# Holding each k copy for a store, and GpSimd's drain for all stores, in a windowed attention kernel

## The chip, the cores and the metric

The kernel runs on one core of a Trainium2 chip. The metric is the device time of that core in microseconds (us), the median of several runs; lower is better. Every run told of here is fast. A single core has no second die to compare with, so fast means that the run lies within 1.5% of the fastest of the same kernel. The runs of the kernel before on one chip agree within 0.13%, and the 95% interval of a ratio below is about ±0.0014, or 1.3 us; a smaller difference between two times isn't clear by itself.

## The reference

Attention within windows of 64 rows; scale is 1536 to the power -0.5:

```
B, S, D, W = 4, 4096, 1536, 64          # q, k, v: float32
logits = einsum('bnwd,bnud->bnwu', q_w, k_w) * scale
attn   = softmax(logits over u)
out    = einsum('bnwu,bnud->bnwd', attn, v_w)   # float32
```

Three inputs of 100.66 MB are read and one output of that size is written. The arithmetic is small beside that.

## The kernel before

A block is 512 rows; there are N = 32. GpSimd asks for all loads but the first q, which are cast to fp16 on the way into SBUF, and for all stores but the last block's, on one DMA queue. When a load has landed, GpSimd copies it to the one buffer that PE reads and asks for the load of two blocks later. PE, the matrix engine, transposes q and k, multiplies them, and multiplies the exponentials with v, reading SBUF and writing PSUM, the two memories on the chip. VectorE and ScalarE copy out of PSUM; their scaled output goes to one of NO = 3 buffers, from which it is stored.

```
    def hand_over(x, u, dst, m, g):
        gp.wait_ge(landed[x][u % NL], 16 * ((u + u % NL) // NL))   # the load has landed
        gp.wait_ge(m, u)                                           # PE is done with the old one
        gp.tensor_copy(out=dst..., in_=landing[x][u % NL]...).then_inc(c_l, 1)
        copies[0] += 1
        gp.wait_ge(c_l, copies[0])
        gp.sem_inc(g, 1)                                           # tell PE
        request(x, u + NL)                                         # the load of block u + 2
...
        for u in range(1, N):
            hand_over("q", u, q16, m_q, g_q)
            hand_over("k", u, k16, m_k, g_k)
            if u + NL == N - 1:
                hand_over("v", u, v16, m_v, g_v)
            gp.wait_ge(m_q, u + 1)
            store(u - 1)                    # adds 16 to d_o[(u - 1) % NO] when landed
            if u + NL != N - 1:
                hand_over("v", u, v16, m_v, g_v)
...     # SyncE issues the two stores of the last block
        gp.drain()
        gp.sem_inc(done, 1)
        sy.wait_ge(done, 1)
        for i in range(NO):                 # SyncE waits for GpSimd's stores
            last = max(u for u in range(N - 1) if u % NO == i)
            sy.wait_ge(d_o[i], 16 * (last // NO + 1))
```

(Cuts are marked with "...", and the comments are added.)

The softmax here doesn't subtract the row's maximum and nothing guards it: scores larger than these inputs give would overflow.

Of the kernel before, what the change touches and what calls it, by code (L numbers as in the profile page):

```python
# [17 lines left out]
def kernel(  # L18
# [20 lines left out]
    N = B * S // UR  # L39
# [11 lines left out]
    def sem(name):  # L51
        sems.append(nc.alloc_semaphore(name))
        return sems[-1]
# [4 lines left out]
    NL = 2  # L58
# [3 lines left out]
    NO = 3  # L62
# [13 lines left out]
    d_o = [sem(f"d_o{i}") for i in range(NO)]  # L76
# [19 lines left out]
    def rows(x, row0, n, r):  # L96
        return x[row0 : row0 + P * n].rearrange("(h p r) d -> p h (r d)", p=P, r=r)

    def slots(t, lo, hi, r):
        return t[:, lo:hi, :].rearrange("p (h r) d -> p h (r d)", r=r)  # L100

    def load(name, u, dst, s):
        src = {"q": qf, "k": kf, "v": vf}[name]
        r = R if name == "v" else SLOTS
        nc.gpsimd.dma_start(
            out=slots(dst, 0, SLOTS, r), in_=rows(src, u * UR, SLOTS, r)
        ).then_inc(s, 16)
# [176 lines left out]
    def store(u):  # L284
        nc.gpsimd.dma_start(
            out=rows(of, u * UR, SLOTS, SLOTS), in_=slots(outs[u % NO], 0, SLOTS, SLOTS)
        ).then_inc(d_o[u % NO], 16)

    def request(x, u):
        if u < N:  # L290
            load(x, u, landing[x][u % NL], landed[x][u % NL])
# [3 lines left out]
    def hand_over(x, u, dst, m, g):  # L295

        gp = nc.gpsimd
        gp.wait_ge(landed[x][u % NL], 16 * ((u + u % NL) // NL))
        gp.wait_ge(m, u)
        gp.tensor_copy(  # L300
            out=dst[:, :, :].bitcast(FP32), in_=landing[x][u % NL][:, :, :].bitcast(FP32)
        ).then_inc(c_l, 1)
        copies[0] += 1
        gp.wait_ge(c_l, copies[0])
        gp.sem_inc(g, 1)
        request(x, u + NL)

    with tc.tile_critical(no_gpsimd_drain=True):

        nc.sync.dma_start(  # L310
            out=slots(outs[0], 0, SLOTS, SLOTS), in_=rows(qf, 0, SLOTS, SLOTS)
        ).then_inc(d_q0, 16)
        load("k", 0, k16, d_k0)
        nc.vector.memset(ident[:, :], 0.0).then_inc(i_d, 1)
        nc.gpsimd.wait_ge(i_d, 1)
        nc.gpsimd.affine_select(
            out=ident[:, :], in_=ident[:, :], compare_op=mybir.AluOpType.not_equal,
            fill=1.0, base=0, pattern=[[-1, P]], channel_multiplier=1,
        ).then_inc(i_p, 1)
        load("v", 0, v16, d_v0)  # L320
        for u in (1, 2):
            for x in "qkv":
                request(x, u)
        nc.gpsimd.wait_ge(d_q0, 16)
        nc.gpsimd.tensor_copy(out=q16[:, :, :], in_=outs[0][:, :, :]).then_inc(c_q, 1)

        nc.vector.memset(ones[:, :], 1.0).then_inc(i_d, 1)
        nc.vector.memset(zeros[:, :], 0.0).then_inc(i_d, 1)
        for et in ets:
            nc.vector.memset(et[:, :, :, :], 0.0).then_inc(i_d, 1)  # L330
        nc.scalar.wait_ge(i_d, 5)
        nc.scalar.activation(zeros[:, 3:4], zeros[:, 0:1], EXP, bias=zeros[:, 0:1], scale=1.0)

        with nc.Fori(0, N, engines=OrderedEngineSet([PE]), head_slot={PE: 0}):
            tensor_unit()
        assert N % NO == 2
        for eng, unit in ((DVE, vector_unit), (ACT, scalar_unit)):
            with nc.Fori(0, N // NO, engines=OrderedEngineSet([eng]), head_slot={eng: 0}):
                for u in range(NO):
                    unit(u)  # L340
            for u in range(N - 2, N):
                unit(u)

        sy = nc.sync
        for j in range(NJ):
            for n in (2, 3):
                sy.sem_inc(f_o[j][n], 1)
        for a in range(2):
            sy.sem_inc(fr[a], NO)
        sy.sem_inc(f_s[-1], 1)  # L350
        sy.wait_ge(i_p, 1)
        sy.wait_ge(i_d, 5)
        sy.wait_ge(c_q, 1)
        sy.sem_inc(g_q, 1)
        sy.sem_inc(g_k, 1)._wait_ge(d_k0, 16)
        sy.sem_inc(g_v, 1)._wait_ge(d_v0, 16)
        for u in range(NO, N):
            sy.wait_ge(d_o[u % NO], 16 * (u // NO))
            for a in range(2):
                sy.sem_inc(fr[a], 1)  # L360

        gp = nc.gpsimd
        for u in range(1, N):
            hand_over("q", u, q16, m_q, g_q)
            hand_over("k", u, k16, m_k, g_k)
            if u + NL == N - 1:

                hand_over("v", u, v16, m_v, g_v)
            gp.wait_ge(m_q, u + 1)
            store(u - 1)  # L370
            if u + NL != N - 1:
                hand_over("v", u, v16, m_v, g_v)


        last = rows(of, (N - 1) * UR, SLOTS, SLOTS)[:, 0, :]
        for i, c in enumerate((1, 3)):
            for a in range(2):
                sy.wait_ge(n_e[a], c)
            sy.dma_start(
                out=last[:, 2 * i * D : 2 * (i + 1) * D],  # L380
                in_=outs[(N - 1) % NO][:, 2 * i : 2 * (i + 1), :].rearrange("p r d -> p (r d)"),
            ).then_inc(d_l[i], 16)
        gp.drain()
        gp.sem_inc(done, 1)
        sy.wait_ge(done, 1)
        for i in range(NO):
            last = max(u for u in range(N - 1) if u % NO == i)
            sy.wait_ge(d_o[i], 16 * (last // NO + 1))
        for i in range(2):
            sy.wait_ge(d_l[i], 16)  # L390
        lo, hi = min(s.num for s in sems), max(s.num for s in sems)
        assert hi - lo + 1 == len(sems)
        sy.sem_clear(range(lo, hi + 1))
# [30 lines left out]
```

## Time and profile before

| | before |
|---|---|
| median, range of 6 runs | 943.35 us, 943.21 to 943.64 |
| span of the profiled run | 941.7 us |
| DMA queue q0, share of 16 engines | 99.7% |
| PE busy | 644.9 us (68%) |
| mean granted PE clock (1 is full speed) | 0.884 |

The prediction below shows the lines that say what bounds the kernel: the DMA queue is full. Three more lines of the page are those of GpSimd's copies. Their columns are line, engine, operation, tiles, shapes and count, then busy time and mean length, then the idle time just before them and what ended most of it:

```profile
L300 POOL COPY v<-vl 128x3072 f32<-128x3072 f32 x31 | 85.2, 2749 | 272.4 <-DMA vl<-in_v_dram 272.4
...
L300 POOL COPY k<-kl 128x3072 f32<-128x3072 f32 x31 | 85.2, 2748 | 102.8 <-DMA kl<-in_k_dram 102.8
L300 POOL COPY q<-ql 128x3072 f32<-128x3072 f32 x31 | 85.0, 2743 | 99.8 <-DMA ql<-in_q_dram 99.8
```

GpSimd waits longest for v, because a store lies between k and v in the queue.

### The profile page before, as it was taken

The page shows a single profiled execution, that of the slowest core. Times are in us where ns is not written, and L with a number is a line of the kernel's source. Part 1 is how long each engine was busy: PE and PEld are TensorE (multiplying, and loading weights), DVE is VectorE, ACT ScalarE, POOL GpSimd, SP SyncE. Part 2 cuts the span into 40 slices and gives each one's busy share as a digit, 9 for nine tenths or more (in the row PEclk, how much of TensorE's full clock was granted, in tenths as well). Part 3 has the DMA queues.
Part 4 walks back from the last instruction along what each step waited for, and adds up shares of the span by engine and source line. Part 5 has one row for each costly group of instructions (what it writes and reads, how often), then busy time and mean ns, then how long its engine had stood idle before and what let it go on. Part 6 is the DMA issues. An engine that isn't in the chain of part 4 may idle for free. (4 is left out here: it accounts for less than half of the span.)

```text
span 941.7 us, 13144 instructions
## 1 busy us (share of the span) xinstructions
PE 644.9 (68%) x5120; PEld 373.5 (40%) x3584; DVE 288.3 (31%) x517; ACT 335.5 (36%) x642; POOL 334.2 (35%) x225
## 2 busy tenths in 40 slices
PE   0877777666766867768666586676776767767683
PEld 0544444433444423445233443334533344334450
DVE  0233333333323332233322233322333223333232
ACT  0344444333333333333333333333333334233331
POOL 4244433344333342333433334333343333443230
PEclk9999999988889788798988999889878889798886
DMA  9999999999999999999999999999999999999997
GB/s 256 219 215 278 265 237 282 283 281 277 231 275 284 280 282 236 266 282 281 283 245 255 283 282 280 256 245 283 282 280 269 233 281 283 282 279 231 273 322 323
DMA packets 22684, 253.35 MB, mean 269 GB/s; under 512 B 2064, under 2 KB 2064, under 8 KB 10256
## 3 DMA queue, kind: packets, MB, share of 16 engines
q0 software_dynamic: 22240, 246.95, 99.7%
q1 hardware_dynamic: 432, 6.29, 1.7%
q14 instruction: 10, 0.08, 0.0%
q8 instruction: 2, 0.03, 0.0%
HBM read 301.99 MB, written 100.66 MB: 428 GB/s over the span
## 5 line engine op out<-in xcount | busy, mean ns | idle before, releaser
L164 PE MATMUL lt<-xq,xk 128*128 128x256 f16 x1536 | 202.6, 281 | 0.0
L300 POOL COPY v<-vl 128x3072 f32<-128x3072 f32 x31 | 85.2, 2749 | 272.4 <-DMA vl<-in_v_dram 272.4
L192 PEld LDWEIGHTS <-et 128*64 128x64 f16 x512 | 40.8, 132 | 331.5 <-issue 317.0
L152 PE MATMUL tp<-ident,q 128*128 128x128 f32 x768 | 109.1, 288 | 80.2 <-DVE xq L228 55.9
L164 PEld LDWEIGHTS lt<-xq,xk 128*128 128x128 f16 x1536 | 152.9, 100 | 26.9
L152 PE MATMUL tp<-ident,k 128*128 128x128 f32 x768 | 125.5, 298 | 54.3 <-PEq L218 37.5
L112 PE MATMUL sp<-ones,et 128*64 128x1 f16 x512 | 52.8, 179 | 146.2 <-PEq L218 126.8
L152 PEld LDWEIGHTS tp<-ident,q 128*128 128x128 f32 x768 | 86.9, 146 | 120.8 <-issue 120.8
L228 ACT COPY xk<-tp 128x512 f32<-128x512 f32 x96 | 59.4, 619 | 199.7 <-ACTq L218 199.7
L152 PEld LDWEIGHTS tp<-ident,k 128*128 128x128 f32 x768 | 96.7, 153 | 71.8 <-issue 69.9
L300 POOL COPY k<-kl 128x3072 f32<-128x3072 f32 x31 | 85.2, 2748 | 102.8 <-DMA kl<-in_k_dram 102.8
L300 POOL COPY q<-ql 128x3072 f32<-128x3072 f32 x31 | 85.0, 2743 | 99.8 <-DMA ql<-in_q_dram 99.8
L245 DVE RECIPROCAL rs<-sp 128x1 f32<-128x1 f32 x128 | 21.3, 166 | 323.9 <-DVEq L218 323.4
L112 PE MATMUL o<-v,et 128*64 128x512 f16 x768 | 118.7, 443 | 0.0
L228 DVE COPY xk<-tp 128x512 f32<-128x512 f32 x96 | 66.4, 692 | 165.4 <-DVEq L218 165.4
L279 ACT ACTIVATE out<-tp,rs 128x512 f32<-128x512 f32 x64 | 44.0, 687 | 177.2 <-ACTq L218 177.2
L269 ACT ACTIVATE et<-lt,zeros 32x128 f16<-32x128 f32 x256 | 91.8, 359 | 39.4 <-ACTq L218 36.1
L228 ACT COPY xq<-tp 128x512 f32<-128x512 f32 x96 | 56.2, 585 | 127.8 <-ACTq L218 127.8
L112 PE MATMUL tp<-v,et 128*64 128x512 f16 x512 | 101.0, 472 | 0.0
L256 DVE TENSOR_SCALAR out<-o,rs 128x512 f32<-128x512 f32 x128 | 90.3, 747 | 28.6 <-DVEq L218 28.1
L228 DVE COPY xq<-tp 128x512 f32<-128x512 f32 x96 | 66.0, 687 | 84.4 <-DVEq L218 84.4
L112 PE MATMUL lt<-v,et 128*64 128x512 f16 x256 | 64.7, 481 | 0.0
(21 smaller groups left out, 217.5 us busy)
## 6 DMA issues: line engine op xcount, KB each, us to landing
out_dram<-out POOLq DMA_DIRECT2D x31, 3072.0 KB, 61.6
ql<-in_q_dram POOLq DMA_DIRECT2D x31, 1536.0 KB, 54.9
kl<-in_k_dram POOLq DMA_DIRECT2D x31, 1536.0 KB, 54.9
vl<-in_v_dram POOLq DMA_DIRECT2D x31, 1536.0 KB, 54.9
out<-in_q_dram SPq DMA_DIRECT2D x1, 3072.0 KB, 16.7
out_dram<-out SPq DMA_DIRECT2D x2, 1536.0 KB, 12.6
k<-in_k_dram POOLq DMA_DIRECT2D x1, 1536.0 KB, 18.0
v<-in_v_dram POOLq DMA_DIRECT2D x1, 1536.0 KB, 24.3
```

What stands on the lines that cost most here:

```text
L112: return nc.tensor.add_instruction(mybir.InstMatmult(name=nc.get_next_instruction_name(), engine=PE, ins=[low(rhs), low(w)], outs=[low(o)] ...
L152: ins = nc.tensor.transpose(tps[g % 2][:, r, j, :], pairs[:, c * P : (c + 1) * P], ident[:, :])
L164: ins = nc.tensor.matmul(lts[h][:, r, :, :], lhsT=keys(c, h, r, w), rhs=queries(c, h, w), start=(c == 0 and w == 0 and r == 0), stop=(c == ...
L192: ld = nc.tensor.ldweights(w[h], tile_position=(0, P // H * h))
L228: copy(out=dst, in_=tps[g % 2][:, :, :, :]).then_inc(f_c[g % 4], 1)
L245: ve.reciprocal(out=rs[:, n : n + 1], in_=sp[:, n : n + 1]).then_inc(n_d, 1)
L256: ins = ve.tensor_scalar_mul(scaled(u, n, j), bank(n, j), scalar1=rs[:, n : n + 1])
L269: ins = sc.activation(ets[h][s, :, :, t], lts[h][s, :, :, t], EXP, bias=zeros[s, 0:1], scale=scale)
L279: ins = sc.activation(scaled(u, n, j), bank(n, j), COPY, bias=0.0, scale=rs[:, n : n + 1])
L300: gp.tensor_copy(out=dst[:, :, :].bitcast(FP32), in_=landing[x][u % NL][:, :, :].bitcast(FP32)).then_inc(c_l, 1)
```

## The change

GpSimd gets a wait before each k copy of blocks 3 to 29: the store that was queued right behind that k must have landed. At the end, the waits for the stores move from SyncE to GpSimd, ahead of its drain, so that GpSimd drains with no store of its own in flight.

```
             hand_over("q", u, q16, m_q, g_q)
+            if NO <= u < N - NL:
+                gp.wait_ge(d_o[u % NO], 16 * (u // NO))
             hand_over("k", u, k16, m_k, g_k)
...
+        for i in range(NO):
+            last = max(u for u in range(N - 1) if u % NO == i)
+            gp.wait_ge(d_o[i], 16 * (last // NO + 1))
         gp.drain()
         gp.sem_inc(done, 1)
         sy.wait_ge(done, 1)
-        for i in range(NO):
-            last = max(u for u in range(N - 1) if u % NO == i)
-            sy.wait_ge(d_o[i], 16 * (last // NO + 1))
```

## The prediction

> **What bounds the kernel now.** I read the page's slices and queues first, to see which resource is never idle; then the timeline of one steady block on GpSimd, to see what each copy waits for; then the tail in stretches of 2 us. A block is 512 rows: 32 blocks, each with a q, a k and a v load and one store of the output.
>
> ```profile
> span 941.7 us, 13144 instructions
> ...
> DMA  9999999999999999999999999999999999999997
> ...
> q0 software_dynamic: 22240, 246.95, 99.7%
> ...
> HBM read 301.99 MB, written 100.66 MB: 428 GB/s over the span
> ```
>
> The sixteen DMA engines are at nine tenths or more in 39 of 40 slices, and GpSimd's one queue q0 fills 99.7% of their time. PE, the busiest compute engine, is at 68%. So this is a transfer-bound kernel, and nothing counts unless it changes how fast the queue moves, lets it run dry, or lengthens an end of the run.
>
> The GpSimd timeline of one block shows the beat of that queue:
>
> ```profile
> 399.06 2.74 POOL L300 COPY q<-ql 128x3072 f32<-128x3072 f32 x1 [3.24 <-DMA ql<-in_q_dram]
> 402.38 0.55 POOL L105 DMA_DIRECT2D ql<-in_q_dram  x1 [0.57 <-POOL q L300]
> 406.39 2.75 POOL L300 COPY k<-kl 128x3072 f32<-128x3072 f32 x1 [3.46 <-DMA kl<-in_k_dram]
> 409.71 0.53 POOL L105 DMA_DIRECT2D kl<-in_k_dram  x1 [0.57 <-POOL k L300]
> 410.23 0.54 POOL L285 DMA_DIRECT2D out_dram<-out  x1
> 420.91 2.75 POOL L300 COPY v<-vl 128x3072 f32<-128x3072 f32 x1 [10.14 <-DMA vl<-in_v_dram]
> ...
> 428.19 2.74 POOL L300 COPY q<-ql 128x3072 f32<-128x3072 f32 x1 [3.23 <-DMA ql<-in_q_dram]
> ...
> 435.52 2.75 POOL L300 COPY k<-kl 128x3072 f32<-128x3072 f32 x1 [3.47 <-DMA kl<-in_k_dram]
> ```
>
> Columns: start, length, instruction, and in brackets the idle time before it with what ended it. Every copy waits for its own landing. Copy to copy: q to k 7.33 us, k to v 14.52, v to q 7.28; a block is 435.52 - 406.39 = 29.13 us. Between k and v the queue holds one more transfer, the store issued just behind that k's request two blocks earlier; so 14.52 is a store plus a load, and the store lands about 14.52 - 7.28 = 7.2 us after k. Each transfer moves 128 x 6144 x 4 B = 3.15 MB on the memory side, 432 GB/s at 7.28 us.
>
> **What the Trainium skill says.** "DMA: Bandwidth & Descriptors", section "Where 436 GB/s comes from", gives 435.2 GB/s as the ceiling of the SBUF ports; the trace's 432 agrees and leaves under 1%. The same page, "Issuing engines are not separate DMA queues", says that DMAs of all issuers run on the same 16 engines; the last two stores, issued by SyncE, do overlap with GpSimd's last one here. "Perfetto Trace Analysis", "DMA Instruction — SWDGE (GPSIMD)", says that the profiled span of a GpSimd DMA is descriptor generation, not data movement; the trace agrees: 0.5 to 0.7 us per issue against tens of us to landing.
>
> ```profile
> out_dram<-out POOLq DMA_DIRECT2D x31, 3072.0 KB, 61.6
> ql<-in_q_dram POOLq DMA_DIRECT2D x31, 1536.0 KB, 54.9
> kl<-in_k_dram POOLq DMA_DIRECT2D x31, 1536.0 KB, 54.9
> vl<-in_v_dram POOLq DMA_DIRECT2D x31, 1536.0 KB, 54.9
> ```
>
> The last figure is the median time from issue to landing. A transfer takes 7.3 us, so a request stands behind about 54.9 / 7.3 = 7.5 transfers: the backlog is nearly two blocks.
>
> **The change, part by part.**
>
> Part 1, the new wait before the k copy, in blocks 3 to 29 (27 times). For block u it waits for the store of block u-3, which is exactly the one queued right behind block u's k. It adds no data and changes no order: GpSimd issues the same transfers in the same sequence. It moves the k copy from k's landing to that store's landing, about 7.2 us later (406.4 to 413.6 in the block shown). What follows from it:
> - The next k request goes out at 416.9 instead of 409.7 and the store behind it at about 417.5 instead of 410.2. Their landings don't move, as the queue before them doesn't. So k's issue to landing should fall from 54.9 to about 54.9 - 7.2 = 47.7 us, the store's from 61.6 to about 54.4; q and v stay at 54.9. A backlog of 47 us is still over six transfers. Cost: 0.
> - The v copy isn't late: GpSimd is done with k and two issues at about 418.0, and v lands at 420.9. The wait moves from v to k: the page's 102.8 us before the k copies should become about 102.8 + 27 x 7.2 = 297, and the 272.4 before the v copies about 272.4 - 194 = 78.
> - PE gets k 7.2 us later. Does it fit in the block? From the same block's timeline of all engines: end of k copy (409.14) to the end of the exponentials (420.67) is 11.5 us; the product with v runs from 423.98 to the first q transpose at 432.34, 8.4; the q transposes run 403.04 to 408.07, and with the last copy out of PSUM to 408.85, 5.8. Sum 25.7 against 29.13: about 3.4 us of slack, and the loop keeps up with the queue. PE's work just moves: today it waits 5.5 us for v and 1.4 us for k (its waits in this block); afterwards the product with v should start when the exponentials end, near 428.0 instead of 424.0, and PE should wait 3 to 4 us before the k transposes. Cost: 0.
>
> Beginning: the early blocks are the ones where PE lags. In block 3, k lands at 86.0, so its store lands near 93, but that block's q transposes end only at 100.64, where the store behind them is issued (the wait of 10.80 us before it). Block 4: store near 122.4, q transposes done at 125.46. The wait is covered. In block 5 the k copy comes at about 151.5, q is done at 148.87, and the slack takes it. Cost: 0.
>
> End: blocks 30 and 31 have no new wait. Block 29's k copy starts near 851.4 instead of 844.22, so its exponentials end near 851.4 + 2.75 + 11.5 = 865.7, and its product with v, which today starts at 861.95, slips 3.7 us. Its slack, and 4.5 us that PE waits today for v of block 30, take that up before block 31: by 888.07 + 2.75 = 890.8 (v of block 30 copied) the delay is about 1 us, by block 31's k nothing. Cost: 0 to 0.5.
>
> Part 2, the waits moved from SyncE to GpSimd ahead of its drain. Today GpSimd drains right after its last copy, 909.92 + 2.75 = 912.7, with three stores still in the queue. Then it will wait for its last store, issued at 905.96 and landing 29.4 us later, at about 935.4. The queue is busy to about 936:
>
> ```profile
> 924.00:926.00 2.00, 1.52 (x16) 0.14 (x2) 1.27 (x3) 1.61 (x3) 0.00 (x0) 1.00 1.00 430
> ...
> 934.00:936.00 2.00, 0.00 (x0) 0.00 (x0) 0.00 (x0) 0.00 (x0) 0.00 (x0) 0.50 0.85 363
> 936.00:938.00 2.00, 0.00 (x0) 0.00 (x0) 0.00 (x0) 0.00 (x0) 0.00 (x0) 0.50 0.17 74
> 938.00:940.00 2.00, 0.00 (x0) 0.00 (x0) 0.00 (x0) 0.00 (x0) 0.00 (x0) 0.50 0.06 25
> ```
>
> (stretch, length, busy time of PE, weight loads, VectorE, ScalarE and GpSimd, then clock, DMA share and GB/s.) SyncE's own last stores, issued at 924.9 and 927.1, take 12.6 us and land near 939.7. So the drain has about 4 us in which it is hidden. No row shows its cost, and no page bears on the drain of a GpSimd that has DMAs out. Cost: 0, perhaps 1 us if it is slow. Nothing is won either, as SyncE waits for the same stores today.
>
> Sum: 0 + 0 + 0 to 0.5 + 0 to 1. I take +0.2: 943.6 us.
>
> **The rivals.**
> 1. The k delay becomes the bound. If all of it stood in the path, 27 x 7.2 = 194 us, so about 1138. For it: k feeds PE, and the wait is in every block. Against: PE waits 6.9 us per block now and the chain sums to 25.7 of 29.13. If my chain were short by 4 us the loss would be 0.6 x 27 = 16 us, still under 2%.
> 2. The queue runs dry, because k and stores are asked for later. For it: the issue really is late. Against: 47 us of backlog where one transfer takes 7.3. It would show as DMA slices under 9.
> 3. The transfers go faster, because GpSimd's copy and issue fall elsewhere. The skill's ceiling bounds it: 402.65 MB / 435.2 GB/s = 925 us (an estimate) without start and tail, while 2% off 943.4 is 924.6. Faster by over 2% is ruled out; 1 to 3 us would be possible.
> 4. The drain after the stores becomes the last thing. If it took over 4 us the end would move by the excess: 1 to 3 us.
>
> **Range and chances.** The three runs before span 0.4 us. Rivals 2 to 4 at their likely sizes give -1 to +2: 942.5 to 945.2. Rival 1 at full size gets most of the 2% for slower; 1% for faster is for what I haven't thought of.
>
> **What would show it.** Right: DMA slices all at 9, a block of 29.1 us, the k wait near 297 and the v wait near 78, k's landing near 47.7. Step "the chain fits" is wrong if blocks are longer than 29.2 and DMA slices fall to 8. Step "the tail absorbs it" is wrong if SyncE's last stores go out later than 927. Step "the drain is hidden" is wrong if the span goes on over 2 us past the last landing. What would make the number wrong is a change of the rate at which the same queue moves, which nothing here foretells.

## The result, and the profile after

The changed kernel takes 945.61 us (median of 6 runs, 945.54 to 946.04) against 943.35. The ratio is 1.0024, with a 95% interval of 1.0011 to 1.0037. By the 2% rule the two are the same; but the loss of 2.3 us is outside the range that was forecast, and clear of noise.

From the page of the changed kernel, the lines that answer to those shown of before:

```profile
span 944.3 us, 13143 instructions
...
DMA  9999999999999999999999999999999999999996
...
q0 software_dynamic: 22240, 246.95, 99.5%
...
HBM read 301.99 MB, written 100.66 MB: 426 GB/s over the span
...
L300 POOL COPY k<-kl 128x3072 f32<-128x3072 f32 x31 | 85.2, 2750 | 304.6 <-DMA out_dram<-out 291.2
...
L300 POOL COPY q<-ql 128x3072 f32<-128x3072 f32 x31 | 85.1, 2745 | 99.3 <-DMA ql<-in_q_dram 99.3
L300 POOL COPY v<-vl 128x3072 f32<-128x3072 f32 x31 | 85.3, 2753 | 83.6 <-DMA vl<-in_v_dram 83.6
...
out_dram<-out POOLq DMA_DIRECT2D x31, 3072.0 KB, 54.7
ql<-in_q_dram POOLq DMA_DIRECT2D x31, 1536.0 KB, 55.1
kl<-in_k_dram POOLq DMA_DIRECT2D x31, 1536.0 KB, 47.6
vl<-in_v_dram POOLq DMA_DIRECT2D x31, 1536.0 KB, 55.2
```

The wait went where it was expected: 304.6 us before k, nearly all ended by a store ("out_dram<-out"), and 83.6 before v. No slice of DMA time fell below 9 before the last. The queue is still full, carries the same packets, and took longer over them.

GpSimd's timeline of the same block shows the k copy 8.0 us later (it was at 406.39), q and v 0.75 us later:

```profile
399.81 2.74 POOL L300 COPY q<-ql 128x3072 f32<-128x3072 f32 x1 [3.23 <-DMA ql<-in_q_dram]
403.13 0.55 POOL L105 DMA_DIRECT2D ql<-in_q_dram  x1 [0.58 <-POOL q L300]
414.41 2.75 POOL L300 COPY k<-kl 128x3072 f32<-128x3072 f32 x1 [10.73 <-DMA out_dram<-out]
...
421.66 2.75 POOL L300 COPY v<-vl 128x3072 f32<-128x3072 f32 x1 [2.86 <-DMA vl<-in_v_dram]
...
428.94 2.74 POOL L300 COPY q<-ql 128x3072 f32<-128x3072 f32 x1 [3.23 <-DMA ql<-in_q_dram]
```

I followed the start of the q copy through all blocks of both traces. The changed kernel is 0.75 us late at block 14, 2.15 at block 28 and 2.51 at block 31. So the loss isn't at the end of the run: it builds up. Up to block 14 it comes in two jumps (about 0.5 us in block 4, at whose start it was 0.37 early, and 0.6 in block 7). From about block 15 on, a block takes about 29.3 us in place of 29.13. The kernel before begins to do the same, but only at block 21.

What grows is the lag of one DMA engine. A transfer is split over sixteen engines, and the trace keeps the sixteen completions of each. Here are those of block 31's q load (worked out from the trace, in us from the span's start):

| | first of 16 | median | last but one | last |
|---|---|---|---|---|
| before | 891.99 | 892.46 | 894.16 | 895.29 |
| after | 892.02 | 892.99 | 895.16 | 897.80 |

The last moved by 2.51 us, as much as the q copy that waits for it, the median by 0.53 and the first by 0.03. A wait for a transfer needs all sixteen, so the one that trails sets the time. The tail shows it too. In stretches of 2 us, the last two columns are the mean share of the sixteen DMA engines and their GB/s. The changed kernel:

```profile
934.00:936.00 2.00, 0.00 (x0) 0.00 (x0) 0.00 (x0) 0.00 (x0) 0.00 (x0) 0.50 0.94 399
936.00:938.00 2.00, 0.00 (x0) 0.00 (x0) 0.00 (x0) 0.00 (x0) 0.00 (x0) 0.50 0.32 135
938.00:940.00 2.00, 0.00 (x0) 0.00 (x0) 0.00 (x0) 0.00 (x0) 0.00 (x0) 0.50 0.07 31
940.00:942.00 2.00, 0.00 (x0) 0.00 (x0) 0.00 (x0) 0.00 (x0) 0.00 (x0) 0.50 0.07 31
```

A share of 0.06 is one engine of sixteen. It moves data alone for 4 us. The line of before for 938 to 940, shown in the prediction, says 0.06 as well: I had read it as the end of the queue and not as one engine by itself.

The packets say where it falls behind. Between 250 and 780 us of the trace's clock, load packets take 474 ns (v) and 926 ns (q, k) in both kernels, alike to 0.05 ns in the mean. Store packets usually take 912 ns, and the first of each engine 925. Of 2304 in that stretch, 50 took over 2% more than 912 before, and 82 after. In the stores of late blocks nearly all of these slow packets follow one another end to start, so they are one engine's. I call what a store's 128 packets take over 912 ns, the 925s left out, its **excess**, and give the mean over the stores of blocks 6 to 25: 128 ns before, 193 after. The difference of 65 ns over the 27 blocks with the wait is 1.8 us of the 2.3 lost. (The same sum, the excess less 128 ns times 27, comes within 0.7 us of what each of the fourteen runs below gained or lost.) The jump of 0.6 us in block 7 comes with slow load packets in that one profile. The profile of e1 below has one of 0.4 a block earlier; whether it comes in every run isn't known.

### The profile page after: what moved, and what is told of

It reads as the page before. It is cut to its first block, busy times and chain, and to the rows that moved or that the text cites. A ratio compares the mean times of both kernels' runs of the same rounds, so it can differ in the third digit from the quotient of the medians.

```text
span 944.3 us, 13143 instructions
## 1 busy us (share of the span) xinstructions
PE 639.5 (68%) x5120; PEld 395.4 (42%) x3584; DVE 287.9 (30%) x517; ACT 334.9 (35%) x642; POOL 334.6 (35%) x225
## 5 line engine op out<-in xcount | busy, mean ns | idle before, releaser
L152 PE MATMUL tp<-ident,k 128*128 128x128 f32 x768 | 150.3, 341 | 126.2 <-PEq L218 117.0
L164 PE MATMUL lt<-xq,xk 128*128 128x256 f16 x1536 | 213.8, 291 | 0.0
L300 POOL COPY k<-kl 128x3072 f32<-128x3072 f32 x31 | 85.2, 2750 | 304.6 <-DMA out_dram<-out 291.2
L152 PEld LDWEIGHTS tp<-ident,k 128*128 128x128 f32 x768 | 116.3, 177 | 146.9 <-issue 144.3
L164 PEld LDWEIGHTS lt<-xq,xk 128*128 128x128 f16 x1536 | 158.9, 103 | 32.2
L152 PE MATMUL tp<-ident,q 128*128 128x128 f32 x768 | 107.1, 284 | 80.2 <-DVE xq L228 56.4
L192 PEld LDWEIGHTS <-et 128*64 128x64 f16 x512 | 38.4, 112 | 232.1 <-issue 156.3
L300 POOL COPY v<-vl 128x3072 f32<-128x3072 f32 x31 | 85.3, 2753 | 83.6 <-DMA vl<-in_v_dram 83.6
L112 PE MATMUL sp<-ones,et 128*64 128x1 f16 x512 | 50.5, 167 | 82.5 <-ACT et L269 74.2
L112 PE MATMUL o<-v,et 128*64 128x512 f16 x768 | 102.3, 394 | 0.0
L228 DVE COPY xq<-tp 128x512 f32<-128x512 f32 x96 | 66.0, 688 | 83.6 <-DVEq L218 83.6
L112 PE MATMUL tp<-v,et 128*64 128x512 f16 x512 | 81.7, 387 | 0.0
L256 DVE TENSOR_SCALAR out<-tp,rs 128x512 f32<-128x512 f32 x64 | 48.1, 751 | 32.4 <-DVEq L218 32.4
## 6 DMA issues: line engine op xcount, KB each, us to landing
out_dram<-out POOLq DMA_DIRECT2D x31, 3072.0 KB, 54.7
kl<-in_k_dram POOLq DMA_DIRECT2D x31, 1536.0 KB, 47.6
```

Source lines behind the costliest of these rows:

```text
L112: return nc.tensor.add_instruction(mybir.InstMatmult(name=nc.get_next_instruction_name(), engine=PE, ins=[low(rhs), low(w)], outs=[low(o)] ...
L152: ins = nc.tensor.transpose(tps[g % 2][:, r, j, :], pairs[:, c * P : (c + 1) * P], ident[:, :])
L164: ins = nc.tensor.matmul(lts[h][:, r, :, :], lhsT=keys(c, h, r, w), rhs=queries(c, h, w), start=(c == 0 and w == 0 and r == 0), stop=(c == ...
L192: ld = nc.tensor.ldweights(w[h], tile_position=(0, P // H * h))
L228: copy(out=dst, in_=tps[g % 2][:, :, :, :]).then_inc(f_c[g % 4], 1)
L256: ins = ve.tensor_scalar_mul(scaled(u, n, j), bank(n, j), scalar1=rs[:, n : n + 1])
```

## The experiments

The theory is that the wait makes the trailing engine's stores slower. The rivals are the moved drain (B), the later issue of k and store (A2), and GpSimd's copy falling at another place (A3, later C). Each run's ratio is against runs of the kernel before on the same chip. The whole list, with the excess from each trace, and PE's mean busy time in the 5 us from 3.5 to 8.5 us after a store's first packet, over the same twenty stores (there the trailing engine moves much of the later part of its share, though in e6 and e9 half of the slow packets start more than 9 us after the store's first):

| run | what it is | us | ratio | excess, ns | PE busy of 5 us |
|---|---|---|---|---|---|
| before | | 943.35 | | 128 | 3.12 |
| after | both parts | 945.61 | 1.0024 | 193 | 3.51 |
| e1 | the k wait alone | 945.66 | 1.0023 | 196 | 3.41 |
| e2 | the moved waits alone | 943.39 | 0.9999 | 132 | 2.94 |
| e3 | only PE late, to the store's landing | 942.00 | 0.9985 | 63 | 2.20 |
| e4 | only the requests late | 943.31 | 0.9999 | 106 | 2.95 |
| e5 | e3, PE 2 to 3 us later | 944.53 | 1.0011 | 150 | 3.23 |
| e6 | e3, PE held until v has landed | 948.80 | 1.0058 | 342 | 3.90 |
| e7 | the k copy held until v has landed | 945.90 | 1.0026 | 210 | 3.24 |
| e8 | e3 without the wait for the store | 941.41 | 0.9978 | 50 | 1.84 |
| e9 | e6, output copies cut | 949.35 | 1.0061 | 356 | 3.89 |
| e10 | after, copies of transposes cut | 945.40 | 1.0020 | 169 | 3.62 |
| e11 | e8, ten matmuls beside the store | 943.98 | 1.0006 | 144 | 4.28 |
| e12 | e8, ten matmuls beside the loads | 941.01 | 0.9975 | 16 | 1.88 |
| e13 | before, one store and load swapped at the end | 943.57 | 1.0000 | 129 | 2.98 |
| e14 | e8 without that swap | 942.07 | 0.9984 | 48 | 1.87 |

### Which part, and which side of it: e1 to e4

```
e1:  the wait before hand_over("k", ...), the end as before
e2:  the waits moved ahead of gp.drain(), no wait before k
e3:  hand_over("k") for blocks 3 to 29, after the copy:
         request("k", u + NL); gp.wait_ge(m_q, u + 1); store(u - 1)
         gp.wait_ge(d_o[u % NO], 16 * (u // NO))
         gp.sem_inc(g_k, 1)                      # PE is told last
e4:      gp.sem_inc(g_k, 1)                      # PE is told first
         gp.wait_ge(d_o[u % NO], 16 * (u // NO))
         request("k", u + NL)                    # the store follows
```

> The new wait before the k copy alone, the end as in the kernel before. Theory A (the wait makes the trailing DMA engine read its stores more slowly, so every later landing slips): about 945.6 us, the last v copy starting near 912.4, the last transfer's 16 completions spread over about 6.6 us. Rival B (the waits moved to GpSimd ahead of its drain lengthen the end): 943.4 us, like the kernel before.

> Only the waits moved from SyncE to GpSimd ahead of the drain; no wait before the k copies. Theory A: 943.4 us, last v copy near 909.9, completions spread over about 4.6 us. Rival B: about 945.6 us.

> k is copied and the next k asked for as in the kernel before, but PE is told of k only when the store behind it has landed. Theory A1 (it is the later phase of PE, VectorE and ScalarE against the stores that slows the trailing engine): 945 to 946 us, late blocks of about 29.30 us. Rival A2 (it is the later issue of k and of the store, that is when descriptors are written): 943.4 us, blocks of about 29.20. Rival A3 (it is GpSimd's copy falling beside the v load): 943.4 us.

> k is copied and handed to PE as in the kernel before; only the next k load and the store are asked for after the store behind k has landed. Theory A1 (PE's phase): 943.4 us, blocks of about 29.20. Rival A2 (late issue): 945 to 946 us, blocks of about 29.30. Rival A3 (GpSimd's copy): 943.4 us.

e1 measured 945.66 and e2 943.39 us: the whole loss is the k wait, and the moved waits with the drain cost nothing that can be measured. e4 gave 943.31: asking later costs nothing that can be measured, as predicted, and A2 falls. e3 fitted no expectation. Telling PE late, by itself, made the kernel **faster** (942.00), and its excess fell to 63 ns. So PE's place against the stores matters, but not as "later is worse".

### The phase, moved further: e5 to e8

```
e5:  e3, between the wait for the store and sem_inc(g_k): four small tensor_copy of a pad tile (2.00 us)
e6:  e3, with gp.wait_ge(landed["v"][u % NL], ...) in place of the wait on d_o
e7:  before, with that wait for v ahead of hand_over("k", ...)
e8:  e3 without gp.wait_ge(d_o[...]): PE is told once k and the store are asked for
```

> e3_pe_late with four small copies on GpSimd between the landing of the store and telling PE of k (some 2 to 3 us, about what the k copy takes in the changed kernel). So PE, VectorE and ScalarE run in the phase of the changed kernel, while k is copied and the next k asked for as early as in the kernel before. Theory P (what slows the trailing engine's stores is the phase of PE's transposes and their copies out of PSUM against the store): slower again, 945 to 946 us. Rival C (it is that GpSimd's k copy no longer falls beside the store): about 942, as e3_pe_late.

> As e3_pe_late, but PE is told of k only when v has landed, another 7.2 us later, so that the product with v and not the transposes should fall beside the store. Theory P: 942 us or a little less, as fewer transposes fall beside the store. Rival C: about 942, no different from e3_pe_late. Both would be wrong if the PE chain doesn't fit: then blocks grow over 29.3 us.

> The kernel before with the k copy, and all behind it, held until v has landed rather than the store: the same kind of wait as in the changed kernel, twice as long. Theory P: the transposes leave the store's time, so 942 to 943 us, faster than the changed kernel in spite of the longer wait. Rival C (no GpSimd copy beside the store): 945.6 or more. A plain loss from lateness would give more than the changed kernel's 945.6.

> As e3_pe_late without its wait for the store: PE is told of k some 4.5 us after k's landing, once the next k and the store are asked for, instead of at 7.3 us (e3) or 2.9 us (kernel before). Theory W (the trailing engine's store packets are slowed by on-chip work beside them, and PE's idle hole of some 3.4 us per block should lie in the store's time): 942 us or less. Rival T (it is the wait on the store's semaphore in itself that made e3 faster): 943.4, as before.

e5 lost all that e3 had won (944.53; that it is over the kernel before isn't clear, ratio 1.0011, interval 0.9997 to 1.0024), with GpSimd's copy in its early place. That speaks against rival C as the whole cause. But e5 stays 1.1 us under the changed kernel: PE is told about 0.7 us earlier in its block there, and the copy's place may have a part. e6 is the slowest correct kernel, 948.80 us with an excess of 342 ns, although its k copy too lies beside the store. Its blocks grew to 29.47 us, the sign given for a PE chain that doesn't fit; but its queue stays full (99.2%, DMA slices at 9), GpSimd's copies wait for landings alone, and the excess by itself makes up the loss. C as the whole cause falls there; but so does the detail in theory P that transposes are the harm. In e6 the product with v fills the store's time and the store suffers most. e7's loss also speaks against the transposes, though its size doesn't decide between the rest. e8 turns e3's gain, which no theory had forecast, into a test: PE is told of k about 4 us after its landing, and the hole in PE's work falls into the store. It came out at 941.41 us, under the kernel before and under e3. The wait on the store's semaphore isn't needed for it.

One engine trails in e6 as in the changed kernel, by more:

```profile
940.00:942.00 2.00, 0.00 (x0) 0.00 (x0) 0.00 (x0) 0.00 (x0) 0.00 (x0) 0.50 0.85 356
942.00:944.00 2.00, 0.00 (x0) 0.00 (x0) 0.00 (x0) 0.00 (x0) 0.00 (x0) 0.50 0.07 31
944.00:946.00 2.00, 0.00 (x0) 0.00 (x0) 0.00 (x0) 0.00 (x0) 0.00 (x0) 0.50 0.03 12
```

In e8 no engine is left alone for so long at the end. The stretch after the one at 0.19 moves nothing:

```profile
936.00:938.00 2.00, 0.00 (x0) 0.00 (x0) 0.00 (x0) 0.00 (x0) 0.00 (x0) 0.50 0.19 80
938.00:940.00 2.00, 0.00 (x0) 0.00 (x0) 0.00 (x0) 0.00 (x0) 0.00 (x0) 0.50 0.00 0
```

### Whose work: e9 and e10

```
e9:   e6;    scaled output copies write 64 of 512 columns
e10:  after; copy(out=dst[:, :, :, 0:16], in_=tps[g % 2][:, :, :, 0:16])
```

Both give a wrong result. The unwritten parts are zeroed at the start (one output buffer holds the first q instead).

> e6_pe_at_v (948.8 us, the slowest) with VectorE's and ScalarE's scaled copies of the output cut to 64 of 512 columns, so the result is wrong on purpose; the stores carry the same bytes and PE does the same matmuls. If it is VectorE's and ScalarE's writes to SBUF beside the store that slow the trailing engine, the loss goes: 942 to 944 us. If it is PE's reads, or the phase alone, it stays: 947 us or more.

> The changed kernel with the copies of the transposes out of PSUM cut to 16 of 128 columns (the result is wrong on purpose), PE's transposes and products unchanged. If VectorE's and ScalarE's writes to SBUF beside the store are the cause: 942 to 943.5 us. If PE's reads are: 945 us or more.

Neither recovered: 949.35 and 945.40 us. VectorE's and ScalarE's writes to SBUF aren't the main cause; the excess of e10 did fall from 193 to 169 ns, so a small part can be theirs. In e9 VectorE's busy time in the 5 us halves against e6 (0.99 against 1.89 us) and the excess stays, 356 against 342 ns; PE's is 3.89 against 3.90.

### The test of cause: e11 and e12

Ten matmuls with a discarded result, in e8, once between the q and the k transposes (beside the store) and once after the last product with k (beside loads):

```
            transpose(g)
+           if g == DC - 1: filler(10)        # e11
...
+       filler(10)                            # e12, before the wait for v
        await_(nc.tensor, g_v)
# filler: nc.tensor.matmul(ops[0][:, :], lhsT=x[:, 0:P], rhs=x[:, 0:512], ...), x = xq[:, 0, :] as fp16
```

> e8_pe_after_ask (941.4 us, PE idle while most of the store runs) with ten extra matmuls of 512 columns on PE per block, put into that idle hole; their result is thrown away, nothing else changes and no other engine gets work. Theory W (PE's work beside the store slows one DMA engine): the packets of a store over their usual 912 ns add up to 100 ns or more per store instead of 50, and the time goes to 942.5 or more. Rival (the phase counts for another reason): 941.4 us and about 50 ns.

> The control of e11: the same ten matmuls after the last product with k, where PE waits for v and loads are running, not the store. Theory W: 941.4 us and about 50 ns per store, as e8. If extra work on PE costs time anywhere: more, like e11.

PE's timeline of one block in e8, with the hole of 2.89 us in front of the k transposes:

```profile
406.60 1.06 PE L152 MATMUL tp<-ident,q 128*128 128x128 f32 x8 [0.55 <-DVE xq L228]
410.56 3.16 PE L152 MATMUL tp<-ident,k 128*128 128x128 f32 x12 [2.89 <-PEq L218]
```

The same in e11, where the hole is filled:

```profile
406.93 1.07 PE L152 MATMUL tp<-ident,q 128*128 128x128 f32 x8 [0.55 <-DVE xq L240]
407.84 2.32 PE L181 MATMUL o<-xq 128*128 128x512 f16 x10
410.33 1.06 PE L152 MATMUL tp<-ident,k 128*128 128x128 f32 x8 [0.17 <-PEq L230]
```

And in e12, where the hole remains and the ten come after the products:

```profile
405.35 1.06 PE L152 MATMUL tp<-ident,q 128*128 128x128 f32 x8 [0.55 <-DVE xq L239]
410.13 3.16 PE L152 MATMUL tp<-ident,k 128*128 128x128 f32 x12 [3.71 <-PEq L229]
...
417.18 2.88 PE L164 MATMUL lt<-xq,xk 128*128 128x256 f16 x24
419.90 2.32 PE L181 MATMUL o<-xq 128*128 128x512 f16 x10
```

The k transposes start no later in e11 than in e8, so nothing on PE is delayed. Yet e11 takes 943.98 us with 144 ns of excess, and e12 941.01 with 16. The same 2.32 us of PE work costs 2.6 us in all beside the stores, and nothing beside the loads. This is the step from "goes together" to "causes".

One thing besides the ten matmuls differs. After the hole PE's granted clock was 0.50 during the k transposes of the blocks shown of e8 and e12; without the hole, in e11, it was 1.00 (twelve transposes take 3.16 us there, eight take 1.06 here). So e11 tests more PE work and faster PE work at once.

The kept traces tell more, packet by packet. In the stores of blocks 6 to 25 that have a slow packet, I joined packets end to start into the eight of that engine (232 such chains in the sixteen traces), and left the 925s out. The first of the eight took its usual 925, and the second wasn't slowed: 0.1 ns over 912 in the mean of 231, and 0.2 where PE was busy over nine tenths of it. From the third on it depends on PE:

| PE during the packet | packets | mean over 912 ns |
|---|---|---|
| busy under a tenth of it | 234 | 2.7 |
| busy over nine tenths, granted clock 0.5 | 87 | 17.6 |
| busy over nine tenths, granted clock 1.0 | 393 | 45.0 |

So it is PE's work beside the later part of an engine's share that goes with the slow packets, and more so at the full clock. (The other engines' work differs between these packets too, so this table by itself shows no cause.)

### A slip of mine, and its control: e13 and e14

e3, e5, e6, e8, e9, e11 and e12 issue block 28's store ahead of block 31's v load, where the kernel before has them the other way round.

```
e13:  before; for every u: store(u - 1), then hand_over("v", ...)
e14:  e8 for blocks 3 to 28 only, so that block 29 keeps the old order
```

> The kernels e3, e5, e6, e8, e11 and e12 also ask for block 28's store ahead of block 31's v, where the kernel before asks for that v first. This run makes that one swap alone in the kernel before. If the swap accounts for the gain of e8 (2.2 us): 941.4 us. If PE's place beside the stores does: 943.4 us, at most 0.5 us less.

> e8_pe_after_ask with block 29 left as in the kernel before, so that block 31's v is asked for ahead of block 28's store again. If PE's place beside the stores gives e8 its gain: 941.4 to 942 us. If the swap does: 943.4 us.

The swap alone gives nothing (943.57 us, ratio 1.0000). e8 with the old order still gains (942.07, ratio 0.9984, interval 0.9970 to 0.9997), but less than e8. So about 1.5 us of e8's gain are PE's place; the other 0.7 may come with the swap, with block 29 itself, or from chance, as the intervals of e8 and e14 overlap. Comparisons among the seven kernels that share the order aren't touched. Nothing beats the kernel before by 2%; e8 is the best useful one, at 0.9978.

### What stays open

The loss follows PE's work beside the stores, but not in a fixed ratio: e11 has PE busy for 4.28 of the 5 us and 144 ns of excess, e6 3.90 and 342. Part of that may be the fixed 5 us, which miss the late packets of e6, and part the clock, which was 1.00 in those 5 us of the changed kernel, 0.88 before. What in PE's work does it isn't settled, nor why an engine's second packet is spared, why one engine bears it, or which: the trace doesn't number the engines. Nor is GpSimd's part. With PE busy over nine tenths, packets from the third on were 15.8 ns over 912 where GpSimd was copying throughout (96 packets) and 47.1 where it wasn't (314). The changed kernel has no GpSimd copy beside the store; no run moves that copy alone.

## Why the prediction was wrong

**What bounds the kernel** was right: the queue, and no compute engine.

**Part 1, waits and backlog**: right to about a tenth. k's time from issue to landing became 47.6 us (47.7 forecast), the store's 54.7 (54.4); the wait before k 304.6 (297), before v 83.6 (78). The store lands rather 7.5 us after k in the mean ((304.6 - 102.8) / 27) than 7.2. That the later requests cost nothing was shown by e4.

**Part 1, PE's chain fits**: right. PE's idle time before the k transposes is 3.47 us in the block shown in the prediction (forecast 3 to 4). Blocks 9 to 14 of the changed kernel still take 29.13 us each. The sign I gave for a failure of this step, blocks over 29.2 with DMA slices at 8, came half true: late blocks are longer, with slices at 9. It couldn't tell a late PE from a slow queue.

**Beginning and end**: the tail was right in substance. SyncE's last stores went out at 927.7 and after in place of 924.9, so the sign given for a failure of this step (later than 927) came true; but the last v copy was already 2.51 us late, and the last of these stores landed 2.53 us late. The tail itself added next to nothing. Whether the jumps in blocks 4 and 7 belong to the wait is open.

**Part 2, the drain is hidden**: right, e2 shows 0.0 us. The trace has the drain itself: begun with all of GpSimd's stores landed, it took 3.25 us in the changed kernel and ended at 940.71, 2.2 us ahead of the last landing (942.91). So it used 3.25 of some 5.5 us of room (about 4 were forecast). Before, it was begun at 912.8 and ended 1.64 us after GpSimd's last store had landed.

**The ceiling in rival 3** was misread. The 432 GB/s count bytes on the memory side, and the ceiling that is cited is one of the SBUF ports. A load is cast to half its size there (1536 KB in the page's issues, 216 GB/s in 7.28 us); only the stores are as large on both sides. So the trace doesn't show that loads stood at that ceiling, and the bound drawn from it (no gain over 2%) isn't shown either. (And 2% off 943.4 is 924.5.)

**The step that failed** is the one in part 1 that says "Their landings don't move, as the queue before them doesn't", with its "Cost: 0". It took a transfer's time as a constant of the queue. Order and bytes didn't move, but moving PE's work by 7 us put other PE work beside the stores, at a higher clock, and one engine's store packets take longer there. Its term was 0 and measured 2.3 us (e1). Rival 3 had a changed rate in mind, but only as a gain; and the closing sentence, that nothing foretells a changed rate, was true of what I had read. The tail's 0.06 and the blocks of 29.2 to 29.3 us at the end of the kernel before could have told me that one engine trails and has no slack.

## What to carry to other kernels

When the DMA queue is the bound and always full, look at the sixteen completions of a transfer and not at the mean share: the slowest engine sets the time, and small losses of that engine add up, block for block. Then a wait that is covered by backlog still isn't free if it shifts compute against a kind of transfer that is sensitive to it. Try the phase with a signal alone, as e3 and e8 do; it costs no buffer, and here it won 1.4 to 2.2 us, where the change lost 2.3.

## What the Trainium skill lacked or had wrong

- "DMA: Bandwidth & Descriptors", section "Latency and other measured facts", says that two DMA engines are usually slower than the rest in traces, and guesses at a clash over SBUF ports. A trailing engine is here too (5.78 us behind the first at block 31's q in the changed kernel, 3.30 before), though the trace can't say which it is. The page doesn't say that PE's work beside a store makes it slower: ten matmuls per block raised the excess per store from 50 to 144 ns and cost 2.6 us (e8 to e11), while beside loads they cost none (e12).
- "Perfetto Trace Analysis", section What "DMA-bound" means, lists "Specific DMA engines" as one of the bounds. To see it, it points to the tracks of the single engines; the trace kept here doesn't number them. What served instead: the share of 0.06 or 0.07 in the tail, and the spread of the sixteen completions (3.30 us before, 5.78 after).
- No page has the cost of GpSimd's drain with stores in flight or without. Here it took 3.25 us after the last store had landed, and begun earlier, as in the kernel before, it ended 1.64 us after that landing; e2 against before is 943.39 to 943.39 us on the same chip.
